# Opening a two-input elementwise kernel with two narrow pieces on two queues, wide pieces behind

## Chip, cores, metric

One core of one Trainium2 chip. The metric is device time in microseconds (us) of one execution. Each ratio is to runs of the kernel before from the same call, and times of different calls are compared through it.

## The reference

```python
# x, y: float32 [1024, 4096]
z = x * y
out = 0.5 * z * (1 + np.tanh(np.sqrt(2 / np.pi) * (z + 0.044715 * z ** 3)))
```

33.55 MB are read, 16.78 MB written. The work is one multiply (VectorE) and one GELU (ScalarE) per element.

## The kernel before

Both arrays are seen as 128 partitions by 32,768 columns, in three pieces, each a contiguous stretch of memory. A narrow piece has 1,280 columns (rows of 5,120 bytes per partition, 640 KB in all), the wide ones 16,384 and 15,104 (rows of 65,536 and 60,416 bytes). SBUF holds all of x, which is overwritten by the product and by the result; y has a buffer of 20,440 columns, so the second wide y load waits until multiplies have released part of it.

```python
PIECES  = [(0, 1280), (1280, 17664), (17664, 32768)]
Y_LOADS = [(1280, 17664, 4056), (17664, 32768, 0), (0, 1280, 15104)]  # from, to, place in the y buffer
Y_FREE  = [0, 3, 4]                         # multiplies to wait for before each y load
STEPS   = [[4096] * 4, [2048] * 7 + [768], [1280]]
STORES  = [(1280, 17664), (17664, 32768), (0, 1280)]
# ... (cut)
_hoist(nc, [load_x(0).ins])                 # SyncE's queue, ahead of the start barrier
_hoist(nc, [load_x(1, nc.scalar).ins])      # ScalarE's queue, ahead of the start barrier
load_y(0)                                   # the rest on SyncE's queue
load_x(2)
for i in range(1, len(Y_LOADS)):
    if Y_FREE[i]:
        nc.sync.wait_ge(sem_mul, Y_FREE[i])
    load_y(i)
# ... (cut: multiply and GELU per step)
for i, (a, b) in enumerate(STORES):
    if i == 0:
        nc.sync.wait_ge(sem_y[-2], 16)      # no store before the wide y load has landed
    nc.sync.wait_ge(sem_act, done[b])
    nc.sync.dma_start(out=columns(out, a, b), in_=xs[:, a:b]).then_inc(sem_o[i], 16)
```

## Time and profile before

| | before |
|---|---|
| median, 6 runs | 119.83 us (119.62 to 119.86) |
| span in the profile | 118.3 us |
| VectorE, ScalarE busy | 30%, 26% |
| DMA queues, share of 16 engines' time | 82.2% + 16.5% |

The transfers fill 98.7% of the time of the 16 DMA engines. A data packet is one row of one partition; what this text calls packet records are the start, length and size of every packet in the trace. One caution on reading them: the profiled execution of this kernel was the fastest of its six, 119.62.

### The profile page before, as it was taken

To read this page: it belongs to the slowest core of one execution; us is meant where nothing else is said; L and a number is where in the kernel's file an instruction comes from. 1 tells how busy PE (TensorE), PEld (TensorE's weight loads), DVE (VectorE), ACT (ScalarE), POOL (GpSimd) and SP (SyncE) were. 2 spreads that over 40 slices of the span, in tenths; PEclk is the share of its full clock that TensorE was granted. 3 is DMA by queue.
4 is the path that set the end of the run, shared out by engine and by line. 5 is a ranking of instruction groups with operands and counts; after the bars stand their busy time and mean duration, and the time that the engine had idled before them with its cause. 6 is when DMAs were issued, how large, how long until landed. Compare 5 with 4: busy or idle time off the path is not lost.

```text
span 118.3 us, 82 instructions
## 1 busy us (share of the span) xinstructions
DVE 35.2 (30%) x13; ACT 31.0 (26%) x14; POOL 0.2 (0%) x4
## 2 busy tenths in 40 slices
DVE  0000000000000069999920000059999940000000
ACT  4000000000000001977974000007998990000000
POOL 0000000000000000000000000000000000000000
DMA  9888899889988897797797797798899889977975
GB/s 493 382 382 382 355 643 421 355 355 532 532 355 355 355 654 327 327 654 327 327 654 327 327 654 327 327 576 355 355 643 421 355 355 429 552 327 327 654 327 222
DMA packets 1296, 50.33 MB, mean 426 GB/s; under 512 B 144, under 2 KB 144, under 8 KB 528
## 3 DMA queue, kind: packets, MB, share of 16 engines
q1 hardware_dynamic: 1152, 41.94, 82.2%
q10 hardware_dynamic: 144, 8.39, 16.5%
HBM read 33.55 MB, written 16.78 MB: 426 GB/s over the span
## 4 chain that ended last, share of the span: by engine, by line
DMA 53%; DVE 24%; ACT 3%; issue 1%; DVEq 0%
DMA ys<-in_y_dram 53%; DVE xs L97 24%; ACT xs L105 3%; DVEq L94 0%
## 5 line engine op out<-in xcount | busy, mean ns | idle before, releaser
L97 DVE TENSOR_TENSOR xs<-xs,ys 128x2048 f32<-128x2048 f32 (+3 forms) x13 | 35.2, 2778 | 60.7 <-DMA ys<-in_y_dram 60.7
L105 ACT ACTIVATE xs<-xs 128x2048 f32<-128x2048 f32 (+3 forms) x13 | 29.7, 2301 | 64.9 <-DVE xs L97 64.9
L105 ACT ACT_TABLE_LOAD x1 | 1.3, 1283 | 1.6 <-PEq L59 1.6
L135 POOL MEMSET const-bfloat16-1.0<- 128x1 bf16 x1 | 0.1, 102 | 0.0
L135 POOL MEMSET const-uint8-127<- 128x1 uint8 x1 | 0.1, 102 | 0.0
L135 POOL MEMSET const-float32-0.0<- 128x1 f32 x1 | 0.1, 99 | 0.2 <-issue 0.2
L135 POOL MEMSET const-float32-1.0<- 128x1 f32 x1 | 0.1, 99 | 0.0
## 6 DMA issues: line engine op xcount, KB each, us to landing
xs<-in_x_dram SPq DMA_DIRECT2D x1, 7552.0 KB, 58.2
ys<-in_y_dram SPq DMA_DIRECT2D x1, 7552.0 KB, 22.5
out_dram<-xs SPq DMA_DIRECT2D x1, 7552.0 KB, 20.4
xs<-in_x_dram SPq DMA_DIRECT2D x1, 640.0 KB, 13.3
ys<-in_y_dram SPq DMA_DIRECT2D x1, 640.0 KB, 19.7
out_dram<-xs SPq DMA_DIRECT2D x1, 640.0 KB, 20.8
xs<-in_x_dram ACTq DMA_DIRECT2D x1, 32.5
ys<-in_y_dram SPq DMA_DIRECT2D x1, 40.7
```

What stands on the lines that cost most here:

```text
L97: nc.vector.tensor_mul(out=xs[:, c : c + w], in0=xs[:, c : c + w], in1=ys[:, r + c - a : r + c - a + w],).then_inc(sem_mul, 1)
L105: nc.scalar.activation(out=xs[:, c : c + w], in_=xs[:, c : c + w], func=GELU).then_inc(sem_act, 1)
L135: nc = _bacc.Bacc("TRN2", target_bir_lowering=False, num_devices=1)
```

## The change

The intent: both inputs open with their contiguous 640 KB piece, each on its own queue, so that a first product can be computed a few microseconds after the start; only wide rows follow. The second y load is split, so that a small piece still covers the turn from loads to stores. The core of the diff:

```diff
-Y_LOADS = [(1280, 17664, 4056), (17664, 32768, 0), (0, 1280, 15104)]
-Y_FREE = [0, 3, 4]
-STEPS = [[4096] * 4, [2048] * 7 + [768], [1280]]
-STORES = [(1280, 17664), (17664, 32768), (0, 1280)]
+Y_LOADS = [
+    (0, 1280, 0),
+    (1280, 17664, 4056),
+    (17664, 31488, 0),
+    (31488, 32768, 13824),
+]
+Y_FREE = [0, 0, 4, 4]
+STEPS = [
+    (0, 0, 1280),
+    *((1, 1280 + 4096 * k, 4096) for k in range(4)),
+    *((2, c, min(2048, 31488 - c)) for c in range(17664, 31488, 2048)),
+    (3, 31488, 1280),
+]
+STORES = [(1280, 17664), (0, 1280), (17664, 32768)]
@@
     _hoist(nc, [load_x(0).ins])
-    _hoist(nc, [load_x(1, nc.scalar).ins])
-    load_y(0)
+    _hoist(nc, [load_y(0, nc.scalar).ins])
+    load_x(1)
+    load_y(1)
     load_x(2)
-    for i in range(1, len(Y_LOADS)):
+    for i in range(2, len(Y_LOADS)):
```

The loop over the steps is rewritten for the new list and does the same work per step.

More of the change, by code (lines that the diff above doesn't have):

```diff
@@ L67, with load_x, load_y @@
     sem_o = [nc.alloc_semaphore(f"sem_o{i}") for i in range(len(STORES))]
-    def load_x(i, engine=nc.sync):
+    def load_x(i):
         a, b = PIECES[i]
-        return engine.dma_start(out=xs[:, a:b], in_=columns(x, a, b)).then_inc(sem_x[i], 16)
-    def load_y(i):
+        return nc.sync.dma_start(out=xs[:, a:b], in_=columns(x, a, b)).then_inc(sem_x[i], 16)
+    def load_y(i, engine=nc.sync):
         a, b, r = Y_LOADS[i]
-        return nc.sync.dma_start(
+        return engine.dma_start(
             out=ys[:, r : r + b - a], in_=columns(y, a, b)
@@ L86 @@
         load_y(i)
-    n = 0
-    done = {}
-    for i, (a, b, r) in enumerate(Y_LOADS):
-        for j, (xa, xb) in enumerate(PIECES):
-            if xa <= a < xb:
-                nc.vector.wait_ge(sem_x[j], 16)
-        nc.vector.wait_ge(sem_y[i], 16)
-        c = a
-        for w in STEPS[i]:
-            nc.vector.tensor_mul(
-                out=xs[:, c : c + w],
-                in0=xs[:, c : c + w],
-                in1=ys[:, r + c - a : r + c - a + w],
-            ).then_inc(sem_mul, 1)
-            n += 1
-            done[c + w] = n
-            nc.scalar.wait_ge(sem_mul, n)
-            nc.scalar.activation(
-                out=xs[:, c : c + w], in_=xs[:, c : c + w], func=GELU
-            ).then_inc(sem_act, 1)
-            c += w
+    seen = set()
+    for n, (i, c, w) in enumerate(STEPS, 1):
+        a, b, r = Y_LOADS[i]
+        if i not in seen:
+            seen.add(i)
+            for j, (xa, xb) in enumerate(PIECES):
+                if xa <= a < xb:
+                    nc.vector.wait_ge(sem_x[j], 16)
+            nc.vector.wait_ge(sem_y[i], 16)
+        nc.vector.tensor_mul(
+            out=xs[:, c : c + w],
+            in0=xs[:, c : c + w],
+            in1=ys[:, r + c - a : r + c - a + w],
+        ).then_inc(sem_mul, 1)
+        nc.scalar.wait_ge(sem_mul, n)
+        nc.scalar.activation(
+            out=xs[:, c : c + w], in_=xs[:, c : c + w], func=GELU
+        ).then_inc(sem_act, 1)
     for i, (a, b) in enumerate(STORES):
@@ L112 @@
             nc.sync.wait_ge(sem_y[-2], 16)
-        nc.sync.wait_ge(sem_act, done[b])
+        nc.sync.wait_ge(sem_act, max(n for n, (_, c, _) in enumerate(STEPS, 1) if a <= c < b))
         nc.sync.dma_start(out=columns(out, a, b), in_=xs[:, a:b]).then_inc(sem_o[i], 16)
```

## The prediction

> **What bounds the kernel now.** I read the page first: busy shares of the compute engines, then section 3 with the DMA queues, then the chain that ended last, then the waits of the queue that issues the transfers, because a kernel that multiplies two arrays and applies one function has little else than transfers to be bound by.
>
> ```profile
> span 118.3 us, 82 instructions
> DVE 35.2 (30%) x13; ACT 31.0 (26%) x14; POOL 0.2 (0%) x4
> q1 hardware_dynamic: 1152, 41.94, 82.2%
> q10 hardware_dynamic: 144, 8.39, 16.5%
> HBM read 33.55 MB, written 16.78 MB: 426 GB/s over the span
> DMA 53%; DVE 24%; ACT 3%; issue 1%; DVEq 0%
> ```
>
> The compute engines work less than a third of the time. The two DMA queues (q1 issued from SyncE, q10 from ScalarE) take 82.2% + 16.5% = 98.7% of what the 16 DMA engines have: 0.987 x 118.3 = 116.8 us of packets on every engine. So only about 1.5 us of the span is anything but transfer. The chain line is a trap here: it gives VectorE 24% of the span, which looks like something to shorten by starting the multiplies earlier. But while VectorE stands in that chain, transfers go on under it. The chain in order of time shows where:
>
> ```profile
> 1.56 40.75 DMA ys<-in_y_dram
> 42.41 13.11 DVE xs L97 x3
> 55.54 22.47 DMA ys<-in_y_dram
> 80.31 13.31 DVE xs L97 x6
> 93.64 3.80 ACT xs L105 x3
> ```
>
> From 42.41 to 55.54 the first three multiplies run and release the y buffer. At 55.54 the second wide y load is issued, but the wide second x load, issued at about 1.95, only lands 58.2 us later, at 60.15 (row below). The queue was still full for another 4 us. The last stretch is the same: multiplies and GELU from 80.31 to 97.4 lie beside the first wide store.
>
> ```profile
> xs<-in_x_dram SPq DMA_DIRECT2D x1, 7552.0 KB, 58.2
> xs<-in_x_dram SPq DMA_DIRECT2D x1, 640.0 KB, 13.3
> ys<-in_y_dram SPq DMA_DIRECT2D x1, 7552.0 KB, 22.5
> ys<-in_y_dram SPq DMA_DIRECT2D x1, 640.0 KB, 19.7
> out_dram<-xs SPq DMA_DIRECT2D x1, 7552.0 KB, 20.4
> out_dram<-xs SPq DMA_DIRECT2D x1, 640.0 KB, 20.8
> ```
>
> The packet records of the trace settle it. Each packet is one row of one partition, 5,120, 60,416 or 65,536 bytes. The first data packet starts at 1.01 us, the last ends at 117.88, the last landing is at 118.25. Counting packets in flight, the 16 engines' mean idle time is 1.12 us in the first 2 us (1.01 of it before the first packet), 0.06 us near 78 to 80 us (between the last loads and the first store), 0.10 us near the very end, 0.06 us from 2 to 6 us, and nothing else that counts. There is no gap in the middle to close.
>
> **What the Trainium skill says.** "DMA: Bandwidth & Descriptors", section "Where 436 GB/s comes from", puts the ceiling of a core's 16 DMA engines at 435 GB/s and a 16 MB transfer at 425. The trace agrees: 426 GB/s over the span, and a 65,536-byte packet takes 2.430 us, 27.0 GB/s, or 432 for 16 engines. The same page, section "Issuing engines are not separate DMA queues", says that transfers started from different engines run on the same 16 DMA engines and interleave. The trace agrees: while both queues had work (to about 32 us) wide packets took about 2.42 us, just as later with one queue. So giving an opening piece "its own queue" adds no bandwidth. Section "Queues, rings and completion order" says each engine takes turns between queue rows packet by packet. The trace shows what that does to a piece of small rows beside one of wide rows: the opening 640 KB of x landed only after 13.3 us, because after its first rows each 0.2 us row waited for a 2.4 us row of the other queue.
>
> **The change part by part.**
>
> 1. Traffic. The same 50.33 MB move. Before: three transfers of 5,120-byte rows, three of 65,536, three of 60,416; each gives each DMA engine 8 rows. Means from the trace are 0.2013, 2.4296 and 2.2319 us, so per engine 24 x 0.2013 + 24 x 2.4296 + 24 x 2.2319 = 4.83 + 58.31 + 53.57 = 116.71 us. Check: first packet to last is 117.88 - 1.01 = 116.87, less 0.16 of gaps. After: the wide second y load is cut into 13,824 and 1,280 columns, that is rows of 55,296 and 5,120 bytes. Estimate for 55,296 bytes, from the two measured sizes (60,416 bytes at 27.07 GB/s, or the line through 5,120 and 60,416): 2.043 us. So 32 x 0.2013 + 24 x 2.4296 + 16 x 2.2319 + 8 x 2.043 = 6.44 + 58.31 + 35.71 + 16.35 = 116.81 us. The change adds 0.10 us of transfer.
>
> 2. The opening. The 640 KB pieces of x and y go out at 0 and 0.12 us, in place of the x piece and the wide x load. Together they are 16 rows x 0.20 = 3.2 us per DMA engine, from 1.0 to about 4.2. The wide x load is issued at 1.56 and needs about 1 us to produce packets (0.0 to 1.01 at the start), so it is there by about 2.6 to 3. No gap, and no gain: the first packet still starts at 1.01, since the first issue is the same. The y piece will probably not land at 4.5 us: its last rows alternate with wide x rows, so I expect 10 to 15 us.
>
> 3. The first multiply. 1,280 columns (1.49 us on VectorE, 1.25 on ScalarE) move from the end to that early point, where nothing waits for them. The four wide ones then wait for 16 narrow and 16 wide rows: 1.01 + 3.2 + 16 x 2.43 = 43.1, plus 0.5 of spread between engines and 0.35 to the landing: 44.0, 1.6 later than the 42.4 of now.
>
> 4. The buffer release. The count awaited rises from 3 to 4, but the first is now the small multiply, so it is again the third wide one: 44.0 + 13.1 = 57.1. Both remaining y loads go out then, at about 57.1 and 57.5. The second wide x load ends on the earliest engine at 43.1 + 8 x 2.23 = 61.0. New packets need about 1 us, so 58.1 against 61.0: 2.9 us in hand (before: 55.54 against 59.3).
>
> 5. From loads to stores. The first store still waits for the wide y load (7.08 MB) to land, which happens at 61.0 + 8 x 2.043 = 77.35 on the first engine and about 78.2 in all, against 78.0 now. The same 640 KB (8 x 0.2 = 1.6 us) lie behind it to cover the issue. The gap of 0.06 us stays.
>
> 6. The end. VectorE has 15,104 columns left instead of 16,384: 17.78 - 2.20 + 0.80 (one 2,048 fewer, 1,536 in place of 768) = 16.4 us, so 94.6, and ScalarE ends about 96.0. Before, the last small store went out at about 97.5. The last store, now the wide one, has to be ready when the first store and the small one are through: that was 98.3 for the first store alone (the second store's first packet, from the packet records), so 98.3 + 1.6 + 0.1 = 100.0. It is issued 4 us before that. Its last packet ends at 117.9 to 118.0, landing 0.4 later.
>
> Sum: +0.10 us of packets, gaps unchanged within 0.1: 119.86 + 0.1 = 119.96.
>
> **The rivals.** (a) The early multiply shortens the path, as the chain's 24% VectorE suggests; 1.49 + 1.25 us of tail work go, so 117.2. Against it: those microseconds lie beside stores now, and 116.7 us of packets plus 1.0 at the start and 0.4 at the end leave no room. (b) A new gap: with all wide loads on one queue the first wide pair lands 1.6 us later and eats the slack of the second y load. It would have to eat 2.9 us more to cost anything; if the release were late by 4.5 us, 1.6 us would be lost, 121.5. (c) Small strided pieces cost more than I take: the opening rows took 0.208 us on average against 0.197 of the later ones; 16 such rows more by 0.011 is 0.2 us, 120.1. The strided 5,120-byte rows of y, read at a pitch of 60,416 bytes, have no counterpart in the trace; twice the time would cost 1.6 us, but the wide reads start at the same pitch and show nothing. (d) A smoother start or end gains the 0.16 us of small gaps: 119.7.
>
> **Range and chances.** Three runs of before lie within 0.06 us, and its profiled run was 119.62, so a change of chip or run is worth some 0.3 us. Terms (c) and (d) add some 0.2 each way. Predicted 119.95, range 119.5 to 120.5. A 2% change is 2.4 us: faster is closed by the packet sum; slower needs (b) or the strided piece at more than its double. Faster 0.01, within 0.975, slower 0.015.
>
> **What would show it right or wrong.** Right: the shares of the two queues still add to 98 to 99% of the span with q10 down to about 3%; wide multiplies start near 44.0; the later y loads go out near 57.1; the last store is issued near 96 and lands at the end; VectorE's share of the chain changes without the time following. Wrong: a stretch between 58 and 62 us or near 78 to 80 with DMA idle, strided rows much over 0.2 us, or a first packet well before or after 1.01 us.

## The result and the profile after

| | before | after |
|---|---|---|
| median, 6 runs each | 119.83 us | 120.47 us (120.43 to 120.59) |
| ratio, 95% interval | | 1.0058 (1.0045 to 1.0071) |

The change costs 0.64 us by the medians: within 2%, but clear of noise, and 0.5 us more than predicted, at the very edge of the range.

The page of the changed kernel, the lines that answer to those of before:

```profile
span 119.1 us, 84 instructions
DVE 35.3 (30%) x13; ACT 31.0 (26%) x14; POOL 0.2 (0%) x4
q1 hardware_dynamic: 1296, 49.68, 97.1%
q10 hardware_dynamic: 144, 0.66, 1.4%
HBM read 33.55 MB, written 16.78 MB: 423 GB/s over the span
DMA 53%; DVE 22%; ACT 4%; issue 1%; SPq 0%; DVEq 0%
```

The shares add to 98.5%, of a longer span: 0.985 x 119.1 = 117.3 us of packets per DMA engine against 116.8. Of the difference, 0.10 us was forecast for the extra rows; the rest means that some packets were slower, and the packet records (below) say which. The last line is the chain by engine: VectorE's share fell from 24% to 22%, and the time rose.

The chain of waits in order of time (start, length, what):

```profile
1.95 42.71 DMA ys<-in_y_dram
44.75 13.11 DVE xs L108 x3
57.87 20.98 DMA ys<-in_y_dram
78.94 1.51 DVE xs L108
81.15 11.10 DVE xs L108 x5
92.28 4.44 ACT xs L114 x3
```

The first wide y load landed at 1.95 + 42.71 = 44.66, where 44.0 was predicted. From there on everything runs to plan: 13.1 us of multiplies, then the y load lands at 78.85, 34.2 us after the first, as in the prediction (78.2 - 44.0). So the loss is all there at 44.66, and the next question is which part of the first 44 us it is. The issues, with the time from issue to landing in the last column:

```profile
xs<-in_x_dram SPq DMA_DIRECT2D x1, 640.0 KB, 4.7
ys<-in_y_dram ACTq DMA_DIRECT2D x1, 640.0 KB, 5.3
xs<-in_x_dram SPq DMA_DIRECT2D x1, 23.7
ys<-in_y_dram SPq DMA_DIRECT2D x1, 42.7
```

The narrow y piece landed after 5.3 us. The prediction had said 10 to 15, because its last rows should have been taking turns with wide rows of x. They did not: the wide rows were not there yet. The packet records agree. The first wide row of each engine starts between 4.37 and 5.33 us, 2.8 to 3.8 us after its load was issued at 1.56, when the last narrow row ends at 5.13 (on most engines sooner). Between 2 and 6 us the 16 engines idle 0.205 us on average (before: 0.058, in its second profile 0.010), and the first 16 wide rows take 2.665 us on average and up to 3.16, where such rows later take 2.418 (the median). (The kernel before has slow first wide rows too, 2.578 us, up to 2.78.)

The second visible difference is at the turn from loads to stores. Busy share of the DMA engines in 40 slices, first of the kernel before, then of the changed kernel, both from 77 to 82 us:

```profile
DMA  0749959959989499990000000000000000999000
```

```profile
DMA  0000143897997998977129990000000000000000
```

Packets count in the slice in which they start, so zeros behind the wide store rows mean nothing. The store rows are the 9s just before the zeros. What counts is the dip ahead of them in the changed kernel (1 2): most engines had run out of narrow load rows before the first store row came. Before, there is no such dip. Counted packet by packet from 78 to 80 us, the gap is 0.31 us per engine against 0.06. It is an obvious suspect, and the first experiments were about it.

### The profile page after: what moved, and what is told of

The parts are those of the page before. It is cut to its first block, busy times and chain, and to the rows that moved or that the text cites. A ratio compares the mean times of both kernels' runs of the same rounds, so it can differ in the third digit from the quotient of the medians.

```text
span 119.1 us, 84 instructions
## 1 busy us (share of the span) xinstructions
DVE 35.3 (30%) x13; ACT 31.0 (26%) x14; POOL 0.2 (0%) x4
## 4 chain that ended last, share of the span: by engine, by line
DMA 53%; DVE 22%; ACT 4%; issue 1%; SPq 0%; DVEq 0%
DMA ys<-in_y_dram 53%; DVE xs L108 22%; ACT xs L114 4%; SPq L81 0%; DVEq L107 0%
```

## The experiments

The theory after this reading (O): the opening leaves the DMA engines late and uneven, and the end is set by the slowest one; the gap near 79 us is the others waiting for it, since the first store waits until all 16 engines have landed the y load. The main rival (S): the gap is itself the loss. Others: the eight extra narrow rows of the split, the strided piece, the order of the stores. Fourteen runs were made, two of them of the kernels already known, for a second profile. All gave correct results.

### e1_no_wait: the gap taken away by removing the store's wait

```diff
-        if i == 0:
-            nc.sync.wait_ge(sem_y[-2], 16)
```

> Changed kernel without the store's wait for the wide y load; the stores then stand in the queue behind the last loads. Theory O (the opening leaves the slowest DMA engine late, and the gap near 79 us is only the other engines waiting for it): the gap of 0.31 us near 79 goes, the engines end further apart (about 0.9 us instead of 0.2), and the time stays within 0.15 us of 120.47. Rival S (the gap at the seam between loads and stores is itself the loss): 0.25 to 0.4 us faster, 120.1 to 120.2.

Measured 121.11 us, ratio to before 1.0101: 1.18 us above before, where the changed kernel was 0.64 above, so about 0.5 us slower than the changed kernel. Both theories missed. The gap did go, yet more than that came in another place: with store rows queued behind them, the last 128 narrow load rows took 0.292 us each on average instead of 0.196, eight rows per engine, so 8 x 0.096 = 0.77 us. The wait that looks superfluous keeps the stores out of the last loads, and is worth having here. This run does not tell O from S, since it added a cost of its own.

### e5_cover: the gap taken away by more cover

```diff
-    (17664, 31488, 0),
-    (31488, 32768, 13824),
+    (17664, 30208, 0),
+    (30208, 32768, 12544),
@@ (the steps follow)
-    (3, 31488, 1280),
+    (3, 30208, 2560),
```

> Changed kernel with the last y piece of 2,560 instead of 1,280 columns, so 3.1 us instead of 1.6 us of loads cover the issue of the first store. Theory O (the slowest DMA engine of the opening sets the end; the gap near 79 us is the others waiting): the gap of 0.31 us goes, the engines end further apart, the time stays at 120.4 to 120.6. Rival S (the gap is itself the loss): 120.1 to 120.2.

Measured 120.36 us, 1.0049 (1.0036 to 1.0063); the changed kernel itself (e8_changed_again) 120.42, 1.005. The busy slices, here from 78 to 81 us, have no dip any more:

```profile
DMA  6969969999696996969999999000000000000000
```

The gap is gone and the time is the same. The engines now land the last store 0.46 us apart instead of 0.19. So the gap was a symptom: engines that are ahead either wait at the turn or finish early, and the slowest sets the end in both cases. S is out. The second profile of the unchanged change (e8_changed_again, below) says the same without any edit.

### e2_open_before: only the opening undone

```diff
     _hoist(nc, [load_x(0).ins])
-    _hoist(nc, [load_y(0, nc.scalar).ins])
-    load_x(1)
+    _hoist(nc, [load_x(1, nc.scalar).ins])
+    load_y(0)
     load_y(1)
```

> Changed kernel with the opening of the kernel before (narrow x piece on SyncE, wide x piece on ScalarE), the narrow y piece following on SyncE; the split of the second y load, the order of computing and of the stores stay as changed. Theory O: 119.8 to 120.0, and the landings of the wide y load spread over 0.5 us instead of 0.95. Rivals T (the eight more narrow rows, the strided piece or the order of the stores cost it): stays at 120.4 to 120.5.

Measured 119.96 us against 119.93 of before, ratio 1.0004 (0.9992 to 1.0016). Its chain:

```profile
1.96 42.17 DMA ys<-in_y_dram
57.34 20.98 DMA ys<-in_y_dram
```

The wide y load lands at 44.12 instead of 44.66. (The cut leaves out that `load_x` takes the issuing engine again.) Everything else of the change is still in this kernel: the split, the strided piece, the narrow product computed first, the order of the stores. Together they cost 0.03 us by the medians, with an interval that allows the predicted 0.10. The loss is in the opening.

### e3_one_queue, e4_wide_first, e6_other_y, e7_x_wide_y_narrow: other openings

```diff
 # e3: both narrow pieces on SyncE's queue
-    _hoist(nc, [load_y(0, nc.scalar).ins])
+    _hoist(nc, [load_y(0).ins])
 # e4: both wide pieces open (SyncE, ScalarE), the narrow ones behind; narrow product after three wide ones
+    _hoist(nc, [load_x(1).ins])
+    _hoist(nc, [load_y(1, nc.scalar).ins])
+    load_x(0)
+    load_y(0)
 # e6: ScalarE opens with columns 31488 to 32768 of y; the y piece (0, 1280) is loaded and used last
 #     (buffer places, multiplies waited for, steps and order of stores follow)
 # e7: wide x piece opens on SyncE, narrow y piece on ScalarE, narrow x piece behind
+    _hoist(nc, [load_x(1).ins])
+    _hoist(nc, [load_y(0, nc.scalar).ins])
+    load_x(0)
```

> Changed kernel with both narrow pieces issued from SyncE, one after the other, no queue of its own for y. If the loss comes from two queues of narrow rows taking turns at once: back to about 119.9 to 120.1. If it comes from narrow rows having to fill the start at all (slow first rows, and issue of the next load close behind): 120.4 or more.

Measured 120.34 us, but from 120.02 to 120.99, ratio 1.0042 (1.0022 to 1.0061). It lies between the two forecasts, and its profile is of its slowest run, so it is inconclusive in size; one queue is no cure.

> Changed kernel with both wide pieces opening, one on each queue, and the narrow pair behind them; the narrow product is computed after three wide ones. Theory O: the narrow rows are out of the opening, so 119.7 to 120.0, near the kernel before. If the cost is of 32 instead of 24 narrow rows per engine wherever they stand: stays near 120.4.

Measured 120.34 us, 1.0031 (1.0018 to 1.0044). The narrow load rows near 41 us, outside the opening, took exactly 0.196 us each, so they cost nothing there. But the opening wide rows were slow instead: the first 16 took 3.14 us on average, those that started in the first 8 us 2.66 and up to 3.43, which adds 0.72 us per engine. O in its first form, "narrow rows in the opening are the trouble", is too simple.

> Changed kernel in which ScalarE opens with the last 1,280 columns of y (rows 60,416 bytes apart) and the y piece that belongs to the opening x piece comes last. If the loss comes from reading x and y at the same offset of their arrays at the same time: 119.9 to 120.1. If any two narrow pieces in the opening cost it: 120.4 to 120.6.

Measured 120.35 us, 1.0042 (1.0029 to 1.0055). Reading x and y at the same offset at the same time is not the cause.

> Changed kernel with the wide x piece opening on SyncE and the narrow y piece on ScalarE, the narrow x piece behind. If one narrow and one wide piece side by side are the good opening, whichever tensor and queue they have: 119.9 to 120.05, landings of the wide y load about 0.5 us apart. If the x array or SyncE's queue has to give the narrow piece: 120.3 or more.

Measured 120.31 us, 1.0038 (1.0026 to 1.0051). One narrow and one wide piece are not enough: here wide rows open on every engine, as in e4_wide_first, and again those of the first 8 us took 2.66 us (the first 16: 3.16). Whether it matters which array or queue gives the narrow piece was not tested apart. What the opening of before has, and these have not, seems to be narrow rows first *and* wide rows that join while narrow ones are still running.

### e8_changed_again, e12_before_again: second profiles

> The changed kernel itself once more, for the same chip and a second profile: 120.4 to 120.6, the landings of the wide y load again 0.7 to 1.0 us apart, narrow rows of the opening again above 0.21 us on average.

Measured 120.42 us, 1.005 (1.0037 to 1.0063). The narrow rows of the opening took 0.216 us, the first 16 wide rows 2.906, idle time from 2 to 6 us 0.19. The turn from loads to stores, 77 to 82 us as above, has no dip like that of the first profile:

```profile
DMA  0000000044998999999967999000000000000000
```

The gap there is 0.05 us instead of 0.31, and the run took 120.50 us. The same kernel is as slow without the gap, so the gap comes and goes from run to run and is not what the change costs. The landings of the wide y load were 0.54 us apart, less than expected: how far the engines fall apart differs from run to run.

> The kernel before once more, for a second profile: its first one was taken in the fastest of its runs (119.62). Expected 119.8 to 120.0, slow first rows somewhat above the 0.28 us per DMA engine of the first profile, landings of the wide y load 0.5 to 0.6 us apart, no idle time between 3 and 6 us.

Measured 119.83 us, 0.9998. Its first 16 wide rows took 2.65 us, idle time 0.01; landings 0.71 apart, more than expected. Its gap at the turn is 0.15 us. So neither the spread nor the gap marks the two kernels; in these four profiles the dry spell from 2 to 6 us and the late landing do.

### e9_y_later: narrow y piece issued after the barrier

```diff
-    _hoist(nc, [load_y(0, nc.scalar).ins])
+    load_y(0, nc.scalar)
```

> Changed kernel with the narrow y piece still on ScalarE's queue, but issued after the start barrier (about 1.6 us) and not at 0.12, so that for the first 1.6 us only narrow x rows are there and the wide x load is issued at the same moment as the narrow y piece. If the loss is two narrow pieces being all that the DMA engines have in the first 4 us: 119.9 to 120.1, no idle time between 2 and 6 us. If it is the narrow y piece on its own queue as such: 120.3 or more.

Measured 121.19 us, from 120.73 to 122.05, 1.0131. Far off the hoped-for side. Now the narrow x rows alone are all the engines have: they last until 3.2 us, the wide x load, issued at 1.45, brings its first rows from 2.88 to 3.78 us (the narrow y rows come only at 5.87, behind them), the idle time from 2 to 6 us is 0.18 and the first 16 wide rows take 2.96 us. This profile is of its fastest run; why others took up to 1.3 us more stays open.

By what was written before it ran, this result speaks for the rival (the narrow y piece on its own queue as such); but e3_one_queue, without such a queue, was slow too. These numbers suggested theory W: wide rows that arrive after the narrow ones have run out, on all engines at about the same time, pay a dry spell and slower first rows than wide rows that join a stream of narrow ones.

### e10_wide_x_sooner: the wide x load issued at 0.42 instead of 1.56

```diff
     _hoist(nc, [load_y(0, nc.scalar).ins])
-    load_x(1)
+    _hoist(nc, [load_x(1).ins])
     load_y(1)
```

> Changed kernel with the wide x load issued right behind the narrow one (about 0.4 us instead of 1.56). If the loss is the wide rows coming too late behind the narrow ones (idle time of 0.13 to 0.2 us between 2 and 6 us): that idle goes and the time falls to 120.0 to 120.2. If it is slow first rows, narrow and then wide, that are each paid: 120.3 to 120.5.

Measured 120.08 us, 1.002 (1.0008 to 1.0033), against 120.42 and 1.005 of e8_changed_again, with nearly the same runs of before. The landing of the narrow y piece shows that its rows now take turns with wide ones:

```profile
ys<-in_y_dram ACTq DMA_DIRECT2D x1, 640.0 KB, 10.2
1.91 42.23 DMA ys<-in_y_dram
```

The first line is its issue (10.2 us to landing, 5.3 in the changed kernel), the second a piece of the chain: the wide y load lands at 44.14. The first 16 wide rows took 2.446 us, the idle time from 2 to 6 us was 0.064. One line moved wins back 0.34 of 0.57 us. The profile is of its fastest run (119.93). And the load that was issued 1.14 us sooner has its first rows only 0.3 us sooner: they start at 4.10 to 4.90 us instead of 4.37 to 5.33.

### e13_before_wide_late and e14_longer_opening: the same from both other sides

```diff
 # e13: kernel before
-    _hoist(nc, [load_x(1, nc.scalar).ins])
+    load_x(1, nc.scalar)
 # e14: changed kernel; opening pieces of 2,560 columns, no issue moved (the steps follow)
-PIECES = [(0, 1280), (1280, 17664), (17664, 32768)]
+PIECES = [(0, 2560), (2560, 17664), (17664, 32768)]
```

> Kernel before with one edit: the wide x piece on ScalarE is issued after the start barrier (about 1.5 us) instead of at 0.12. Theory W (wide rows that come after the narrow rows have run out, on all DMA engines at about the same time, pay a slow first row and a short dry spell): 120.3 or more, first wide rows 2.6 us and over on average, idle time between 2 and 6 us. If wide rows issued late cost nothing and the loss comes from two narrow pieces: 119.85 to 119.95.

Measured 120.7 us, 1.0081 (1.0061 to 1.0101). The kernel before, with nothing but its wide x load issued late, is at least as slow as the changed kernel (1.0058 and 1.005). First 16 wide rows 3.00 us, idle time 0.28. The wide x load lands at 1.44 + 42.47 = 43.91 (the wide pair of before had landed at 42.31, in its second profile at 42.66):

```profile
1.44 42.47 DMA xs<-in_x_dram
```

(This profile is of its slowest run, 121.44; the timing does not depend on that.)

> Changed kernel with opening pieces of 2,560 columns (10,240-byte rows) on both queues and nothing issued sooner: the narrow rows last to about 7.5 us, so the wide x load, issued at 1.56, is there before they run out. Theory W: no dry spell, first wide rows near 2.25 us (60,416 bytes), time like that of the run with the wide x load issued sooner, 120.0 to 120.15. If two narrow pieces in the opening cost it as such: 120.3 to 120.5.

Measured 120.12 us, 1.003 (1.0017 to 1.0043), against before on runs of 119.84. The landings:

```profile
xs<-in_x_dram SPq DMA_DIRECT2D x1, 1280.0 KB, 7.7
ys<-in_y_dram ACTq DMA_DIRECT2D x1, 1280.0 KB, 12.9
1.95 42.27 DMA ys<-in_y_dram
```

Two narrow pieces still open, on two queues, but they last long enough: the last y rows take turns with wide ones (12.9 against 7.7), the first 16 wide rows took 2.229 us, not a nanosecond above what such rows take later, and nothing idled from 2 to 6 us. What remains above before are slow opening rows: the 10,240-byte ones of the first 8 us took 0.428 us on average where later ones of the same size took 0.385 to 0.388, some 0.6 us per engine over the 16 of them. Theory W has three edits in three places behind it, but of unequal weight: e10 and e13 move the time clearly, while the 1.003 of e14 is no better than the 1.0031 of e4_wide_first. What e14 shows is that the dry spell and the slow wide rows go when the opening lasts longer, and that slow narrow rows remain.

### e11_both_better: the version the runs point to

It is e2_open_before with the split of e5_cover.

> The version that the runs so far point to: the opening of the kernel before, the split y load of the change with a last piece of 2,560 columns. It keeps the good opening and has no gap before the first store, but the slowest DMA engine still sets the end: 119.8 to 120.0, same as before within 0.2%. Over 0.3% faster would mean that the gap near 79 us is a loss of its own when the opening is good.

Measured 119.94 us, 1.001 (0.9996 to 1.0023). No dip at the turn, and no gain over before: with 117 us of packets in a span of 118.6 there is nothing to win this way. No version beat the kernel before.

## Why the prediction was right or wrong

**The bound: right.** The rival (a) that the early product shortens the path did not come: the multiply did run at 5.53 us, VectorE's share of the chain fell to 22%, and the time rose. The queue shares add to 98.5%, as forecast; that q10 would fall to about 3% was a slip, since only the 8 narrow rows of y are on it, 8 x 0.2 = 1.6 us (1.4% measured).

**Traffic, +0.10: consistent.** e2_open_before carries all of it and is 1.0004 of before. Rows of 55,296 bytes took 2.042 us (2.043 estimated), the strided narrow rows 0.196 us each. Splitting and stride cost nothing beyond the byte count that a timing good to 0.2 us would show. (One check in the prediction is loose: "less 0.16 of gaps" leaves out two of the small gaps that it lists. Nothing rests on it.)

**The opening, part 2: wrong.** The step that failed is "needs about 1 us to produce packets (0.0 to 1.01 at the start), so it is there by about 2.6 to 3. No gap". I took the delay of the very first load of the program, with nothing before it, for that of a third load behind two others. The trace of the kernel before could have warned me: there the second load, wide x, is issued at 0.12, and its first rows start at 2.03 to 2.49, about 2 us later and not 1. Measured for the third load of the changed kernel: 2.8 to 3.8 us after issue. The narrow rows were all but over by then (the last ends at 5.13), which also broke the forecast of 10 to 15 us for the narrow y piece (5.3). The cost of this was put at zero. Its size, from five profiles with this opening (the two of the changed kernel, and those of e1, e5 and e6) against the two with the same transfers and the opening of before (e2, e11), all means per DMA engine up to the landing of the wide y load:

| | opening of the change | opening of before |
|---|---|---|
| idle from 2 to 6 us | 0.16 | 0.02 |
| wide rows above 2.418 us, first 30 us | 0.34 | 0.20 |
| narrow rows above 0.196 us, first 30 us | 0.37 | 0.33 |
| slowest engine behind the mean | 0.37 | 0.26 |
| wide y load landed, slowest engine | 44.58 | 44.12 |

The first four differences add to 0.14 + 0.14 + 0.04 + 0.11 = 0.43; the landing differs by 0.46, and the end (span, without e1, which has a cost of its own) by 0.48. The first two terms are the late wide rows, 0.28 in all; the narrow rows themselves, rival (c), are only 0.04. The split is rough, because single profiles scatter: idle runs from 0.08 to 0.21 in the first group, the wide rows from 0.20 to 0.63 (0.18 and 0.23 in the second group), and the fourth differs widely between profiles of one kernel. That the opening costs the time is shown by e2; how it divides is an estimate.

**Buffer release, part 4: right.** 57.87 to the predicted 57.1, late only by the lateness of the landing; the busy slices show no hole near 61 us, and rival (b) did not come.

**The turn, part 5: 0.31 us of gap instead of 0.06 in the first profile, 0.05 in the second.** Harmless in both: e5_cover shows that closing it brings nothing.

**The end, part 6: right.** From the first store row, at 79.7 us, the changed kernel needs 39.4 us to the last landing; the kernel before needed 118.25 - 78.86 = 39.4 too.

**What stays open.** Why the first rows of an opening are slow at all, narrow (0.87 us at worst for 5,120 bytes) or wide (3.4 at worst). Wide rows that joined running narrow ones took anything from 2.45 us (e10) to 2.58 to 2.65 (the opening of before), late ones from 2.55 to 3.00, so the ranges overlap, and joining helps on average but does not by itself give the size. The runs show when it happens, not what inside the chip does it. Nor is it shown what the wide load waits for between its issue and 4.4 us. It is no fixed delay after the issue: 2.8 to 3.8 us in the changed kernel, 3.7 to 4.5 in e10, where the issue is sooner and the narrow x rows ahead of it in the same queue end at 3.5 to 4.1 us, and 1.4 to 2.3 in e9.

## What to carry to other kernels

Where transfers fill the time, as they did here, starting compute earlier wins nothing; look at what a change does to the DMA engines' first and last microseconds and to the slowest of the 16. Do not open with rows so short that they run out before the next load's rows arrive: issue the long load right behind the short one. That won back 0.34 of 0.57 us here, and a longer opening perhaps as much (1.003 in place of 1.005, from different calls); neither reached the kernel before. To estimate when a load's rows arrive, take a load in the same place in the trace, and not the first one. A gap in front of a wait for all engines can be the shadow of an earlier lateness, so close it in an experiment before you call it the loss.

## What the Trainium skill lacked or had wrong

- "DMA: Bandwidth & Descriptors", section "Latency and other measured facts", gives about 0.6 us to the first byte of a load issued from SyncE or ScalarE. Here the first load of the program took 1.00 to 1.03 us to its first packet, the second of the kernel before, issued at 0.12 us, 1.9 to 2.4, and a wide load issued third, at 1.56 us, 2.8 to 3.8 us. The page says nothing of loads issued closely behind others.
- No page has the slow first rows: the first 16 rows of 65,536 bytes took 2.55 to 3.00 us on average where they came behind narrow rows that had run out, 2.45 to 2.65 where they joined running ones, 3.14 to 3.16 where they opened themselves (e4, e7), and 2.418 later in the same kernels.
- "DMA: Bandwidth & Descriptors", section "Queues, rings and completion order", has the turn-taking between queues, and the trace agrees (the narrow piece of y landed after 10.2 us beside wide rows, 5.3 without). It lacks that narrow load rows slow down when stores are queued behind them: 0.292 us instead of 0.196.
- No page has that a gap in front of a wait for all 16 engines can be harmless (e5_cover: a gap of 0.31 us closed, time unchanged).
